# Score matmuls of a recurrent branch on column tiles of TensorE: 32 keys each, against their own group's queries

## The chip, the cores and the metric

The kernel runs on one core of a Trainium2 chip. The time is that of one execution on the device, in microseconds (us), from a timer outside the profiler; each kernel is run several times and the median is compared. The profile is one more execution, recorded by the hardware profiler: TensorE (PE in the profile; its weight loads, PEld), VectorE (DVE), ScalarE (ACT), GpSimd (POOL), and SyncE (SP), whose queue issues most of the loads.

## The reference, cut to what matters

One block of an encoder: an input projection, a recurrent branch (HGRN2) and an attention branch, a gated merge, and an MLP. The change is in the recurrent branch, 8 heads of 128 channels over 256 tokens:

```python
def hgrn2_scan(q, k, v, log_g):
    ...
    def step(S, inp):
        qc, kc, vc, gc = inp
        b = jnp.cumsum(gc, axis=2)
        o_inter = jnp.einsum('bhtk,bhkv->bhtv', qc * jnp.exp(b), S)
        diff = b[:, :, :, None, :] - b[:, :, None, :, :]
        decay = jnp.exp(jnp.where(causal[:, :, None], diff, -jnp.inf))
        scores = jnp.einsum('bhtk,bhtsk,bhsk->bhts', qc, decay, kc)
        o_intra = jnp.einsum('bhts,bhsv->bhtv', scores, vc)
        ...
```

So a query t meets each earlier key s with a decay of its own per channel. The score matrix of keys against queries is zero where s > t.

## The kernel before

All large products take their weights as float32 from HBM: ACT casts a piece to float32r (`wh`, line 91), DVE takes the rest (`wl`, line 92), and PE multiplies three times (lines 136 to 138) or, for the transposed projections, in the form of lines 178 and 183. Four `wh` and four `wl` buffers let the two engines work ahead of PE.

The recurrent branch goes by units of two heads, `n` = 0 to 3. A unit's scores are made by distance. The decay between two tokens is split at a block's border, which gives a factor to the key and a factor to the query, so that a plain matmul over the 128 channels gives the scores:

- `diagonal` (line 367): a token with itself, and a pair's second token with its first (`kk` against `q`; columns 128 to 191 of a block of `q` hold the odd tokens with their decay).
- `factors(i, B)` and `level(i, B)` for B = 2, 8, 32 (lines 376 and 407): four blocks of B tokens make a group of 4B. `kl` holds the keys, `qr` the queries: for each group 6B columns, the queries of the three later blocks seen from the block before them (3B), of two blocks seen from two before (2B), and of one block seen from three before (B).
- `level128` (line 443): the second 128 tokens against the first.

For the diagonal and the levels a unit has four blocks of 128 tokens (2 heads, NM = 2 blocks each). Before, each block is one float32 matmul of all its 128 keys against its 192 query columns (lines 371 and 415). This gives every key against every group's queries, and only the key's own group is wanted. DVE takes those out of PSUM: at the diagonal a product with the identity (line 372) and a predicated copy (line 373), at a level three predicated copies for each head (line 422), under masks that GpSimd builds at the start (line 271). They all write the score matrix `sd`, 128 keys by 128 queries for each block, which is the stationary operand of the output matmuls (line 479).

The order on PE is written in the code. The projections go on all the time, and each of their weight pieces calls `tick` (line 145), which counts down to the next entry of a list `behind`: `scores` (line 523) puts a unit's seven steps there, a few pieces apart. So a score step stands between two projection matmuls, and PE takes it in that order. The steps are: diagonal and factors of B = 2; factors of 8; level 2; factors of 32; level 8; `factors128`; level 32 and `level128`. On the other engines the scheduler of the language places the instructions.

Tiles with a tag share that tag's buffers: `e` (two) for the exponentials, `qr` (two), `kl` (three), `sm` (two PSUM buffers) for score results.

Of the kernel before, what the change touches and what calls it, by code (L numbers as in the profile page):

```python
# [50 lines left out]
def tile_hybrid_block(  # L51
# [216 lines left out]
    LEVELS = (2, 8, 32)  # L268
    mask1 = hp.tile([P, 64], F32, name="mask1")
    band(mask1, [[-2, 64]], 1)  # L270
    masks = hp.tile([P, len(LEVELS), 192], F32, name="masks")
    for i, B in enumerate(LEVELS):
        v = masks[:, i, :].rearrange("p (n k b) -> p n k b", k=6, b=B)
        for k0, k1 in ((0, 3), (3, 5), (5, 6)):
            band(v[:, :, k0:k1, :], [[-4 * B, 32 // B], [-B, k1 - k0], [0, B]], B)
    reset = hp.tile([P, 2 * T], F32, name="reset")
    nc.gpsimd.memset(reset, 1.0)
    nc.gpsimd.memset(reset.rearrange("p (c t) -> p c t", t=CH)[:, :, 0:1], 0.0)
# [47 lines left out]
    def hq_pair(u, z, g):  # L326

        nc.vector.tensor_tensor(z, z, bc(rstd_t, 1, 2), op=ALU.mult)
        s = h2(f"sq{u}")
        nc.scalar.activation(s, z, AF.Sigmoid)  # L330
        q = hp.tile([P, 2, NM, 192], F32, name=f"q{u}", tag="q", bufs=2)
        half = lambda a: a.rearrange("p h (m t) -> p h m t", t=P)
        nc.vector.scalar_tensor_tensor(q[:, :, :, 0:P], half(z), DK ** -0.5, half(s), op0=ALU.mult, op1=ALU.mult)
        odd = lambda a: a.rearrange("p h m (j u) -> p h m j u", u=2)[:, :, :, :, 1]
        for h in range(2):
            nc.vector.tensor_tensor(q[:, h, :, P:], odd(q[:, :, :, 0:P])[:, h], odd(half(g))[:, h], op=ALU.mult)
        return q

    def v_chunk(g):
# [20 lines left out]
    def hgrn_scores(n, made):  # L360

        kk, b, q = made["kk"], made["b"], made["q"]
        sd = hp.tile([P, 2, NM, P], F32, name=f"sd{n}", tag="sd", bufs=2)
        so = hp.tile([P, 2, P], F32, name=f"so{n}", tag="so", bufs=2)
        held = {}

        def diagonal():
            for h in range(2):
                ps = ps_sm.tile([P, NM, 192], F32, name=f"ps{n}_1{h}", tag="sm")
                for m in range(NM):  # L370
                    nc.tensor.matmul(ps[:, m, :], kk[:, h, m * P:(m + 1) * P], q[:, h, m, :], start=True, stop=True)
                nc.vector.tensor_tensor(sd[:, h], ps[:, :, 0:P], bc(ident, 1, NM), op=ALU.mult)
                nc.vector.copy_predicated(sd[:, h].rearrange("p m (j u) -> p m j u", u=2)[:, :, :, 1],
                                          bc(mask1.bitcast(I32), 1, NM), ps[:, :, P:])

        def factors(i, B):
            npar = 2 * T // (4 * B)
            blocks = lambda a: a.rearrange("p h t -> p (h t)").rearrange("p (n v b) -> p n v b", v=4, b=B)
            bv = blocks(b)
            end = bv[:, :, :, B - 1]  # L380
            el = hp.tile([P, npar, 4, B], F32, name=f"el{n}_{B}", tag="e", bufs=2)
            nc.vector.tensor_tensor(el, bc(end, 3, B), bv, op=ALU.subtract)
            nc.scalar.activation(el, el, AF.Exp)
            er = hp.tile([P, npar, 4, B], F32, name=f"er{n}_{B}", tag="e", bufs=2)
            rr = hp.tile([P, npar, 4], F32, name=f"rr{n}_{B}", tag=f"rr{B}", bufs=2)
            if B < CH // 2:
# [3 lines left out]
                nc.scalar.activation(rr[:, :, 1:3], rr[:, :, 1:3], AF.Exp)  # L390
# [8 lines left out]
            qr = hp.tile([P, npar, 6, B], F32, name=f"qr{n}_{B}", tag="qr", bufs=2)  # L399
            wide = lambda a, k: a.rearrange("p (a n) k b -> p a n (k b)", n=32 // B)[:, :, :, k]  # L400
            qv = q[:, :, :, 0:P].rearrange("p h m t -> p (h m) t").rearrange("p a (n w) -> p a n w", w=4 * B)
            nc.vector.tensor_tensor(wide(qr, slice(0, 3 * B)), qv[:, :, :, B:], wide(er, slice(B, 4 * B)), op=ALU.mult)
            nc.vector.tensor_tensor(qr[:, :, 3:5, :], qr[:, :, 1:3, :], bc(rr[:, :, 1:3], 3, B), op=ALU.mult)
            nc.vector.tensor_tensor(qr[:, :, 5, :], qr[:, :, 4, :], bc(rr[:, :, 1], 2, B), op=ALU.mult)
            held[i] = kl, qr, er, rr

        def level(i, B):
            kl, qr, _, _ = held[i]
            klf = kl.rearrange("p n v b -> p (n v b)")
            qrf = qr.rearrange("p n k b -> p (n k b)")  # L410
            for h in range(2):
                ps = ps_sm.tile([P, NM, 192], F32, name=f"ps{n}_{B}{h}", tag="sm")
                for m in range(NM):
                    a = 2 * h + m
                    nc.tensor.matmul(ps[:, m, :], klf[:, a * P:(a + 1) * P], qrf[:, a * 192:(a + 1) * 192],  # L415
                                     start=True, stop=True)
                dst = sd[:, h].rearrange("p m (n w) -> p m n w", w=4 * B)
                src = ps.rearrange("p m (n w) -> p m n w", w=6 * B)
                mask = masks[:, i, :].rearrange("p (n w) -> p n w", w=6 * B).bitcast(I32)
                for d0, k0, k1 in ((1, 0, 3), (2, 3, 5), (3, 5, 6)):  # L420
                    k = slice(k0 * B, k1 * B)
                    nc.vector.copy_predicated(dst[:, :, :, d0 * B:], bc(mask[:, :, k], 1, NM), src[:, :, :, k])

        def factors128():
            kl, qr, er, rr = held[2]
            heads = lambda a: a.rearrange("p (h m) v b -> p h m v b", m=NM)
            r = rr.rearrange("p (h m) v -> p h m v", m=NM)
            r0, r1 = r[:, :, 0, :], r[:, :, 1, :]
            d128 = small.tile([P, 2, 4], F32, name=f"d128{n}", tag="d128", bufs=2)
            nc.vector.tensor_copy(c128[:, :, 2], r0[:, :, 3])  # L430
            nc.vector.tensor_tensor(c128[:, :, 1], r0[:, :, 2], r0[:, :, 3], op=ALU.mult)
            nc.vector.tensor_tensor(c128[:, :, 0], c128[:, :, 1], r0[:, :, 1], op=ALU.mult)
            nc.vector.tensor_copy(d128[:, :, 1], r1[:, :, 0])
            nc.vector.tensor_tensor(d128[:, :, 2], r1[:, :, 0], r1[:, :, 1], op=ALU.mult)
# [4 lines left out]
            nc.vector.tensor_tensor(ql[:, :, 0, :], q[:, :, 1, 0:32], heads(er)[:, :, 1, 0, :], op=ALU.mult)  # L439
            nc.vector.tensor_tensor(ql[:, :, 1:4, :], heads(qr)[:, :, 1, 0:3, :], bc(d128[:, :, 1:4], 3, 32), op=ALU.mult)  # L440
            held["128"] = kc, ql

        def level128():
# [765 lines left out]
```

## Time and profile before

| | us |
|---|---|
| median of 3 runs | 1388.04 (1387.65 to 1388.07) |
| profiled execution, first to last instruction (span) | 1387.1 |
| PE busy | 1375.5 (99%) |
| DVE busy | 1137.2 (82%) |
| ACT busy | 922.2 (66%) |
| POOL busy | 143.3 (10%) |

The median lies 0.9 us above the span of the profiled execution; the timer counts a little on both sides of the span. PE's busy time is the union of its matmuls from start to modelled end; since matmuls are pipelined, a matmul's length in a row is longer than the time until the next one starts. The chain of waits counts each piece only up to the next one, so it is the chain that shows what a matmul costs in a full stream. A float32 matmul in the program is two matmul records and two weight loads in the trace (64 matmuls of line 415 and 371 stand there as 128 records). Records of 128*128 use the whole array, 128*64 half of its columns, 64*128 half of its rows.

### The profile page before, as it was taken

Reading aid. Unit: us, or ns where it says so; the run is one execution under the profiler, and the core shown is the slowest. Engines: PE = TensorE matmul, PEld = TensorE weight load, DVE = VectorE, ACT = ScalarE, POOL = GpSimd, SP = SyncE. Lnnn points to the kernel's source line nnn. Section 1 sums busy time; section 2 is a strip of 40 time slices with the busy share of each in tenths; the row PEclk is TensorE's granted clock in tenths of the full one; section 3 lists DMA queues with packets and bytes.
Section 4 is the critical chain, followed back from the end, with each engine's and each line's share of the span. In section 5 each row is a group of like instructions: output and inputs, shape, how many; then the busy total and the mean of one; then the engine's idle time right before and its main releaser. Section 6 shows DMA issues by size and latency. Waiting matters only on the chain.

```text
span 1387.1 us, 18586 instructions
## 1 busy us (share of the span) xinstructions
PE 1375.5 (99%) x6550; PEld 1144.4 (83%) x6550; DVE 1137.2 (82%) x1413; ACT 922.2 (66%) x1181; POOL 143.3 (10%) x227
## 2 busy tenths in 40 slices
PE   9999999999999999999999999999999999999997
PEld 7889888878788888888888888888888888888886
DVE  7897988876878785697998977879877888878885
ACT  6765655665676664446777766678666876668864
POOL 3000001100100000001211011200111001110200
PEclk9999999999999999999999999999999999999999
DMA  9644446685669896558979789997899888998892
GB/s 324 240 168 152 154 166 230 178 291 169 163 213 286 260 271 225 187 167 273 295 221 309 247 257 297 264 271 228 251 297 301 243 237 248 276 303 262 261 282 95
DMA packets 124077, 331.61 MB, mean 239 GB/s; under 512 B 11072, under 2 KB 11840, under 8 KB 123600
## 3 DMA queue, kind: packets, MB, share of 16 engines
q1 hardware_dynamic: 103696, 265.59, 54.6%
q0 software_dynamic: 19568, 64.04, 23.5%
q8 instruction: 51, 0.84, 0.2%
q10 hardware_dynamic: 720, 0.81, 0.2%
q14 instruction: 42, 0.34, 0.1%
HBM read 271.67 MB, written 10.49 MB: 203 GB/s over the span
## 4 chain that ended last, share of the span: by engine, by line
PE 96%; DMA 1%; ACT 1%; DVE 1%; issue 0%; SPq 0%; POOLq 0%; POOL 0%; ACTq 0%; DVEq 0%
PE acc_ak L178 2%; PE acc_hf L178 2%; PE acc_hq L178 2%; PE acc_aq L178 2%; PE ps L415 1%; PE acc_hq L183 1%; PE acc_ak L183 1%; PE tp_u L109 1%; PE acc_hf L183 1%; PE acc_hi L137 1%; PE acc_hg L137 1%; PE acc_bb L136 1%; PE acc_ba L138 1%; PE acc_hg L136 1%; PE acc_hi L138 1%; PE acc_hg L138 1%
## 5 line engine op out<-in xcount | busy, mean ns | idle before, releaser
L178 PE MATMUL acc_aq<-act_x,wh_aq 128*128 128x512 f32 x128 | 41.7, 402 | 0.0
L178 PE MATMUL acc_hf<-act_x,wh_hf 128*128 128x512 f32 x128 | 41.1, 403 | 0.0
L178 PE MATMUL acc_hq<-act_x,wh_hq 128*128 128x512 f32 x128 | 40.8, 400 | 0.0
L178 PE MATMUL acc_ak<-act_x,wh_ak 128*128 128x512 f32 x128 | 40.4, 397 | 0.0
L91 ACT CAST wh_bb<-raw_bb 128x1024 fp32r<-128x1024 f32 x16 | 16.9, 1054 | 23.3 <-PE acc_ba L138 17.7
L92 DVE TENSOR_TENSOR wl_bb<-raw_bb,wh_bb 128x1024 fp32r<-128x1024 f32 x16 | 19.6, 1223 | 14.8 <-ACT wh_bb L91 14.8
L91 ACT CAST wh_ba<-raw_ba 128x1024 fp32r<-128x1024 f32 x16 | 16.8, 1053 | 20.5 <-PE acc_bb L138 13.8
L92 DVE TENSOR_TENSOR wl_ba<-raw_ba,wh_ba 128x1024 fp32r<-128x1024 f32 x16 | 19.6, 1224 | 12.2 <-ACT wh_ba L91 12.2
L183 PEld LDWEIGHTS acc_hf<-act_x,wl_hf 128*128 128x128 f32 x128 | 23.4, 188 | 6.5 <-DVE wl_hf L92 1.4
L183 PEld LDWEIGHTS acc_hq<-act_x,wl_hq 128*128 128x128 f32 x128 | 23.4, 188 | 6.2 <-DVE wl_hq L92 1.0
L92 DVE TENSOR_TENSOR wl_aq<-raw_aq,wh_aq 128x1024 fp32r<-128x1024 f32 x16 | 19.5, 1221 | 10.8 <-ACT wh_aq L91 10.8
L91 ACT CAST wh_aq<-raw_aq 128x1024 fp32r<-128x1024 f32 x16 | 16.7, 1051 | 16.8 <-PE acc_hg L138 7.3
L183 PEld LDWEIGHTS acc_ak<-act_x,wl_ak 128*128 128x128 f32 x128 | 23.4, 188 | 5.4 <-issue 0.2
L183 PEld LDWEIGHTS acc_aq<-act_x,wl_aq 128*128 128x128 f32 x128 | 23.4, 188 | 5.0 <-issue 0.2
L183 PE MATMUL acc_aq<-act_x,wl_aq 128*128 128x256 f32 x128 | 25.8, 283 | 0.0
L92 DVE TENSOR_TENSOR act_u<-tp_u,act_u 128x512 fp32r<-128x512 f32 x32 | 21.9, 685 | 4.7 <-ACT act_u L91 4.2
L136 PE MATMUL acc_hg<-wh_hg,act_x 128*128 128x512 f32 x64 | 25.6, 400 | 0.0
L136 PE MATMUL acc_hi<-wh_hi,act_x 128*128 128x512 f32 x64 | 25.5, 399 | 0.0
L183 PE MATMUL acc_hf<-act_x,wl_hf 128*128 128x256 f32 x128 | 24.7, 280 | 0.7 <-DVE wl_hf L92 0.7
L183 PE MATMUL acc_hq<-act_x,wl_hq 128*128 128x256 f32 x128 | 24.7, 279 | 0.6 <-DVE wl_hq L92 0.6
L136 PE MATMUL acc_bb<-wh_bb,act_yb 128*128 128x512 f32 x64 | 25.2, 393 | 0.0
L137 PE MATMUL acc_hi<-wl_hi,act_x 128*128 128x512 f32 x64 | 24.9, 390 | 0.0
(1928 smaller groups left out, 5221.3 us busy)
## 6 DMA issues: line engine op xcount, KB each, us to landing
raw_hi<-in_w_in_n_dram SPq DMA_DIRECT2D x16, 512.0 KB, 3.7
raw_hg<-in_w_in_n_dram SPq DMA_DIRECT2D x16, 512.0 KB, 3.6
raw_aq<-in_w_in_t_dram SPq DMA_DIRECT2D x16, 512.0 KB, 3.8
raw_ak<-in_w_in_t_dram SPq DMA_DIRECT2D x16, 512.0 KB, 4.9
raw_ba<-in_w_branch_a_dram SPq DMA_DIRECT2D x16, 512.0 KB, 4.5
raw_bb<-in_w_branch_b_dram SPq DMA_DIRECT2D x16, 512.0 KB, 4.6
raw_hf<-in_w_in_t_dram SPq DMA_DIRECT2D x12, 512.0 KB, 3.6
raw_hq<-in_w_in_t_dram SPq DMA_DIRECT2D x12, 512.0 KB, 3.7
```

The source lines that it names most:

```text
L91: casts[:] = [(copy or nc.scalar.copy)(hi, src)]
L92: return nc.vector.tensor_tensor(lo, src, hi.bitcast(F32), op=ALU.subtract)
L109: nc.tensor.transpose(tp[:, j, :], src[:, j * P:(j + 1) * P], ident)
L136: nc.tensor.matmul(acc, hi, wh, start=first, stop=False, skip_group_check=True)
L137: nc.tensor.matmul(acc, hi, wl, start=False, stop=False, skip_group_check=True)
L138: nc.tensor.matmul(acc, lo, wh, start=False, stop=last, skip_group_check=True)
L178: nc.tensor.matmul(acc[:, cb, :], wh[:, cb * P:(cb + 1) * P], r.rearrange("p u t -> p (u t)"), start=kt == 0, stop=last)
L183: nc.tensor.matmul(acc[:, cb, 0:T], wl[:, cb * P:(cb + 1) * P], r[:, 0, :], start=False, stop=False)
L415: nc.tensor.matmul(ps[:, m, :], klf[:, a * P:(a + 1) * P], qrf[:, a * 192:(a + 1) * 192], start=True, stop=True)
```

## The change

Every group of 32 keys of a block gets its own matmul, on a column tile of TensorE: its 32 keys are the stationary operand (128 x 32), its own 48 query columns the moving one, and the result goes to that group's 32 partitions of PSUM. `q` is laid out by groups of 32 tokens and 48 columns (`[P, 16, 48]`). At the diagonal and at B = 2 and 8 this gives 16 matmuls of 48 columns in one PSUM tile `[P, 4, 48]`, where there were 4 of 192 columns in two tiles. At B = 32 a group is the whole block; its first three quarters of keys meet 96, 64 and 32 query columns, whose order in `qr` is changed for this (7 slots of 32, in a buffer of its own), so that the results already stand where the score matrix wants them.

DVE's copies for the diagonal, 2 and 8 go into a compact tile `near` (128 x 4 x 32) under compact masks (`own`, `odds`, `steps_in`). `sd` is now two fixed tiles that GpSimd clears once at the start. ACT fills them: four copies from `near` (`placed`), and three copies from PSUM at B = 32, which needs no mask any more.

```diff
-    masks = hp.tile([P, len(LEVELS), 192], F32, name="masks")
-    for i, B in enumerate(LEVELS):
+    masks = hp.tile([P, len(LEVELS) - 1, 192], F32, name="masks", tag="e", bufs=2)
+    for i, B in enumerate(LEVELS[:-1]):
...
+    QUARTERS = [slice(32 * j, 32 * j + 32) for j in range(4)]
...
+    for j, r in enumerate(QUARTERS):
+        nc.gpsimd.tensor_copy(own[r], ident[r, 32 * j:32 * j + 32])
+        nc.gpsimd.tensor_copy(odds[r], mask1[r, 16 * j:16 * j + 16])
+        nc.gpsimd.tensor_copy(steps_in[r], masks[r, :, 48 * j:48 * j + 48])
+    sds = [hp.tile([P, 2, NM, P], F32, name=f"sd{i}", tag=f"sd{i}", bufs=1) for i in range(2)]
+    for sd in sds:
+        nc.gpsimd.memset(sd, 0.0)
...
-        q = hp.tile([P, 2, NM, 192], F32, name=f"q{u}", tag="q", bufs=2)
...
-        for h in range(2):
-            nc.vector.tensor_tensor(q[:, h, :, P:], odd(q[:, :, :, 0:P])[:, h], odd(half(g))[:, h], op=ALU.mult)
+        q = hp.tile([P, 16, 48], F32, name=f"q{u}", tag="q", bufs=2)
...
+        nc.vector.tensor_tensor(q[:, :, 32:48], odd(q[:, :, 0:32]), odd(parts32(g)), op=ALU.mult)
...
+        def quarters(keys, queries, what):
+            ps = ps_sm.tile([P, 4, 48], F32, name=f"ps{n}_{what}", tag="sm")
+            for a in range(4):
+                for j, r in enumerate(QUARTERS):
+                    c = 4 * a + j
+                    nc.tensor.matmul(ps[r, a, :], keys[:, 32 * c:32 * c + 32], queries[:, 48 * c:48 * c + 48], start=True, stop=True)
+            return ps
+
         def diagonal():
-            for h in range(2):
-                ps = ps_sm.tile([P, NM, 192], F32, name=f"ps{n}_1{h}", tag="sm")
-                for m in range(NM):
-                    nc.tensor.matmul(ps[:, m, :], kk[:, h, m * P:(m + 1) * P], q[:, h, m, :], start=True, stop=True)
-                nc.vector.tensor_tensor(sd[:, h], ps[:, :, 0:P], bc(ident, 1, NM), op=ALU.mult)
-                nc.vector.copy_predicated(sd[:, h].rearrange("p m (j u) -> p m j u", u=2)[:, :, :, 1],
-                                          bc(mask1.bitcast(I32), 1, NM), ps[:, :, P:])
+            ps = quarters(kk.rearrange("p h t -> p (h t)"), q.rearrange("p j t -> p (j t)"), "1")
+            nc.vector.tensor_tensor(near, ps[:, :, 0:32], bc(own, 1, 4), op=ALU.mult)
+            nc.vector.copy_predicated(near.rearrange("p a (j u) -> p a j u", u=2)[:, :, :, 1],
+                                      bc(odds.bitcast(I32), 1, 4), ps[:, :, 32:48])
...
+            else:
+                qr = hp.tile([P, npar, 7, B], F32, name=f"qr{n}_{B}", tag="qr32", bufs=1)
...
         def level(i, B):
...
-            for h in range(2):
-                ps = ps_sm.tile([P, NM, 192], F32, name=f"ps{n}_{B}{h}", tag="sm")
-                for m in range(NM):
-                    a = 2 * h + m
-                    nc.tensor.matmul(ps[:, m, :], klf[:, a * P:(a + 1) * P], qrf[:, a * 192:(a + 1) * 192],
-                                     start=True, stop=True)
...
+            if B < 32:
+                ps = quarters(klf, qrf, B)
...
                 for d0, k0, k1 in ((1, 0, 3), (2, 3, 5), (3, 5, 6)):
                     k = slice(k0 * B, k1 * B)
-                    nc.vector.copy_predicated(dst[:, :, :, d0 * B:], bc(mask[:, :, k], 1, NM), src[:, :, :, k])
+                    nc.vector.copy_predicated(dst[:, :, :, d0 * B:], bc(mask[:, :, k], 1, 4), src[:, :, :, k])
+                return
+            ps = ps_sm.tile([P, 4, P], F32, name=f"ps{n}_{B}", tag="sm")
+            for a in range(4):
+                for v, r in enumerate(QUARTERS[:3]):
+                    c = 7 * a + 3 * v
+                    nc.tensor.matmul(ps[r, a, 32 * (v + 1):], klf[:, a * P + 32 * v:a * P + 32 * v + 32],
+                                     qrf[:, 32 * c:32 * (c + 3 - v)], start=True, stop=True)
+            for v, r in enumerate(QUARTERS[:3]):
+                nc.scalar.copy(sd4[r, :, 32 * (v + 1):], ps[r, :, 32 * (v + 1):])
+
+        def placed():
+            for j, r in enumerate(QUARTERS):
+                nc.scalar.copy(sd4[r, :, 32 * j:32 * j + 32], near[r])
...
+        def near_ones():
+            l[1]()
+            placed()
+
...
-        return (sd, so), [first, f[1], l[0], f[2], l[1], factors128, final]
+        return (sd, so), [first, f[1], l[0], f[2], near_ones, factors128, final]
```

In the order of the built program SP's instructions are the same as before. On PE each score step stands between the same two projection matmuls as before. The first one, unit 0's diagonal, stood so before (`ps_10` and `ps_11` are the results of its two heads, `acc_hi` the projection under way):

```order
L138 MATMUL acc_hi_650<-wh_hi_6_706,act_x_108 128x512
L371 MATMUL ps_10_719<-q_646,kk_636 128x192 x2
L371 MATMUL ps_11_724<-q_646,kk_636 128x192 x2
L136 MATMUL acc_hi_650<-wh_hi_6_706,act_x_108 128x512
L137 MATMUL acc_hi_650<-wl_hi_6_707,act_x_108 128x512
```

and stands so now (in the changed kernel's line numbers):

```order
L138 MATMUL acc_hi_659<-wh_hi_6_715,act_x_108 128x512
L384 MATMUL ps_1_728<-q_656,kk_646 32x48 x16
L136 MATMUL acc_hi_659<-wh_hi_6_715,act_x_108 128x512
L137 MATMUL acc_hi_659<-wl_hi_6_716,act_x_108 128x512
L138 MATMUL acc_hi_659<-wh_hi_6_715,act_x_108 128x512
```

Four matmuls over the whole array have become 16 over a quarter of its columns; nothing else moved there.

The second place is ACT at the end of the branch, where unit 3's `level128` result goes to `so` between casts of the next projection's weights (`wh_aq`). Before:

```order
L91 CAST wh_hg_14_2139<-raw_hg_14_2138 128x1024
L91 CAST wh_aq_0_2166<-raw_aq_0_2165 128x1024
L91 CAST wh_aq_4_2207<-raw_aq_4_2206 128x1024
L449 COPY so_1916<-ps_128_2128 128x256
L91 CAST wh_aq_8_2248<-raw_aq_8_2247 128x1024
```

and now:

```order
L91 CAST wh_hg_14_2277<-raw_hg_14_2276 128x1024
L455 COPY sd_421<-near_2021 32x4x32 x2
L91 CAST wh_aq_0_2304<-raw_aq_0_2303 128x1024
L455 COPY sd_421<-near_2021 32x4x32 x2
L91 CAST wh_aq_4_2345<-raw_aq_4_2344 128x1024
L451 COPY sd_421<-ps_32_2250 32x4x96
L451 COPY sd_421<-ps_32_2250 32x4x64
L451 COPY sd_421<-ps_32_2250 32x4x32
L482 COPY so_2020<-ps_128_2266 128x256
L91 CAST wh_aq_8_2386<-raw_aq_8_2385 128x1024
```

ACT's seven new copies of the unit stand between the casts; the casts keep their order.

More of the change, by code (lines that the diff above doesn't have):

```diff
@@ L275, in tile_hybrid_block @@
             band(v[:, :, k0:k1, :], [[-4 * B, 32 // B], [-B, k1 - k0], [0, B]], B)
+    QUARTERS = [slice(32 * j, 32 * j + 32) for j in range(4)]
+    own = hp.tile([P, 32], F32, name="own")
+    odds = hp.tile([P, 16], F32, name="odds")
+    steps_in = hp.tile([P, len(LEVELS) - 1, 48], F32, name="steps_in")
+    for j, r in enumerate(QUARTERS):
[5 more added lines that the diff above has]
+        nc.gpsimd.memset(sd, 0.0)
     reset = hp.tile([P, 2 * T], F32, name="reset")
@@ L330, in hq_pair @@
         nc.scalar.activation(s, z, AF.Sigmoid)
-        q = hp.tile([P, 2, NM, 192], F32, name=f"q{u}", tag="q", bufs=2)
-        half = lambda a: a.rearrange("p h (m t) -> p h m t", t=P)
-        nc.vector.scalar_tensor_tensor(q[:, :, :, 0:P], half(z), DK ** -0.5, half(s), op0=ALU.mult, op1=ALU.mult)
-        odd = lambda a: a.rearrange("p h m (j u) -> p h m j u", u=2)[:, :, :, :, 1]
-        for h in range(2):
-            nc.vector.tensor_tensor(q[:, h, :, P:], odd(q[:, :, :, 0:P])[:, h], odd(half(g))[:, h], op=ALU.mult)
+        q = hp.tile([P, 16, 48], F32, name=f"q{u}", tag="q", bufs=2)
+        parts32 = lambda a: a.rearrange("p h (j t) -> p (h j) t", t=32)
+        nc.vector.scalar_tensor_tensor(q[:, :, 0:32], parts32(z), DK ** -0.5, parts32(s), op0=ALU.mult, op1=ALU.mult)
+        odd = lambda a: a.rearrange("p j (t u) -> p j t u", u=2)[:, :, :, 1]
+        nc.vector.tensor_tensor(q[:, :, 32:48], odd(q[:, :, 0:32]), odd(parts32(g)), op=ALU.mult)
         return q
@@ L362, in hgrn_scores @@
         kk, b, q = made["kk"], made["b"], made["q"]
-        sd = hp.tile([P, 2, NM, P], F32, name=f"sd{n}", tag="sd", bufs=2)
+        sd = sds[n % 2]
+        sd4 = sd.rearrange("p h m t -> p (h m) t")
         so = hp.tile([P, 2, P], F32, name=f"so{n}", tag="so", bufs=2)
+        near = hp.tile([P, 4, 32], F32, name=f"near{n}", tag="near", bufs=2)
         held = {}
-        def diagonal():
-            for h in range(2):
-                ps = ps_sm.tile([P, NM, 192], F32, name=f"ps{n}_1{h}", tag="sm")
-                for m in range(NM):
-                    nc.tensor.matmul(ps[:, m, :], kk[:, h, m * P:(m + 1) * P], q[:, h, m, :], start=True, stop=True)
-                nc.vector.tensor_tensor(sd[:, h], ps[:, :, 0:P], bc(ident, 1, NM), op=ALU.mult)
-                nc.vector.copy_predicated(sd[:, h].rearrange("p m (j u) -> p m j u", u=2)[:, :, :, 1],
-                                          bc(mask1.bitcast(I32), 1, NM), ps[:, :, P:])
+        def quarters(keys, queries, what):
[5 more added lines that the diff above has]
+            return ps
+        def diagonal():
+            ps = quarters(kk.rearrange("p h t -> p (h t)"), q.rearrange("p j t -> p (j t)"), "1")
+            nc.vector.tensor_tensor(near, ps[:, :, 0:32], bc(own, 1, 4), op=ALU.mult)
+            nc.vector.copy_predicated(near.rearrange("p a (j u) -> p a j u", u=2)[:, :, :, 1],
+                                      bc(odds.bitcast(I32), 1, 4), ps[:, :, 32:48])
         def factors(i, B):
@@ L398, in factors @@
             nc.vector.tensor_tensor(kl, blocks(kk), el, op=ALU.mult)
[L399 to L404, printed above, removed]
+            if B < 32:
+                qr = hp.tile([P, npar, 6, B], F32, name=f"qr{n}_{B}", tag="qr", bufs=2)
+                wide = lambda a, k: a.rearrange("p (a n) k b -> p a n (k b)", a=16)[:, :, :, k]
+                qv = q[:, :, 0:32].rearrange("p a (n w) -> p a n w", w=4 * B)
+                nc.vector.tensor_tensor(wide(qr, slice(0, 3 * B)), qv[:, :, :, B:], wide(er, slice(B, 4 * B)), op=ALU.mult)
+                one, two, three, far = qr[:, :, 1:3, :], qr[:, :, 3:5, :], qr[:, :, 4, :], qr[:, :, 5, :]
+            else:
+                qr = hp.tile([P, npar, 7, B], F32, name=f"qr{n}_{B}", tag="qr32", bufs=1)
+                qv = q[:, :, 0:32].rearrange("p (a v) t -> p a v t", v=4)
+                nc.vector.tensor_tensor(qr[:, :, 0:7:3, :], qv[:, :, 1:4, :], er[:, :, 1:4, :], op=ALU.mult)
+                one, two, three, far = qr[:, :, 3:7:3, :], qr[:, :, 1:5:3, :], qr[:, :, 4, :], qr[:, :, 2, :]
+            nc.vector.tensor_tensor(two, one, bc(rr[:, :, 1:3], 3, B), op=ALU.mult)
+            nc.vector.tensor_tensor(far, three, bc(rr[:, :, 1], 2, B), op=ALU.mult)
             held[i] = kl, qr, er, rr
@@ L410, in level @@
             qrf = qr.rearrange("p n k b -> p (n k b)")
-            for h in range(2):
-                ps = ps_sm.tile([P, NM, 192], F32, name=f"ps{n}_{B}{h}", tag="sm")
-                for m in range(NM):
-                    a = 2 * h + m
-                    nc.tensor.matmul(ps[:, m, :], klf[:, a * P:(a + 1) * P], qrf[:, a * 192:(a + 1) * 192],
-                                     start=True, stop=True)
-                dst = sd[:, h].rearrange("p m (n w) -> p m n w", w=4 * B)
-                src = ps.rearrange("p m (n w) -> p m n w", w=6 * B)
-                mask = masks[:, i, :].rearrange("p (n w) -> p n w", w=6 * B).bitcast(I32)
+            if B < 32:
+                ps = quarters(klf, qrf, B)
+                dst = near.rearrange("p a (n w) -> p a n w", w=4 * B)
+                src = ps.rearrange("p a (n w) -> p a n w", w=6 * B)
+                mask = steps_in[:, i, :].rearrange("p (n w) -> p n w", w=6 * B).bitcast(I32)
                 for d0, k0, k1 in ((1, 0, 3), (2, 3, 5), (3, 5, 6)):
                     k = slice(k0 * B, k1 * B)
-                    nc.vector.copy_predicated(dst[:, :, :, d0 * B:], bc(mask[:, :, k], 1, NM), src[:, :, :, k])
+                    nc.vector.copy_predicated(dst[:, :, :, d0 * B:], bc(mask[:, :, k], 1, 4), src[:, :, :, k])
[11 more added lines that the diff above has]
+                nc.scalar.copy(sd4[r, :, 32 * j:32 * j + 32], near[r])
         def factors128():
```

4 lines of the change are left out of this document (2 added, 2 removed).

## The prediction

> **What bounds the kernel now.** The page first: busy shares, and the chain that ended last.
>
> ```profile
> PE 1375.5 (99%) x6550; PEld 1144.4 (83%) x6550; DVE 1137.2 (82%) x1413; ACT 922.2 (66%) x1181; POOL 143.3 (10%) x227
> ...
> PE 96%; DMA 1%; ACT 1%; DVE 1%; issue 0%; SPq 0%; POOLq 0%; POOL 0%; ACTq 0%; DVEq 0%
> ```
>
> PE is busy 99% of the span and is 96% of the chain. So the time is the sum of what PE streams; the question is what the change does to that sum, in the stretch where the score matmuls stand, and whether anything else is close behind PE there. The busy time by windows (span from:to, length, then busy time of PE, PEld, DVE, ACT and POOL, clock, DMA share, GB/s):
>
> ```profile
> 55.00:100.00 45.00, 45.00 (x212) 38.17 (x211) 44.05 (x93) 34.30 (x46) 0.00 (x0) 1.00 0.51 175
> 55.00:215.00 160.00, 160.00 (x835) 139.22 (x834) 142.48 (x312) 101.84 (x132) 2.38 (x2) 1.00 0.47 161
> ```
>
> From 55 to 215 us PE is never idle, at a granted clock of 1.00; DVE is at 89%, ACT at 64%, the DMA engines at 0.47. In the first 45 us of it DVE is at 98%. The chain of waits in one score step (start, length until the next piece, what):
>
> ```profile
> 111.36 0.46 PE acc_hf L178 x2
> 111.82 0.23 PE acc_hf L183 x2
> 112.06 1.30 PE ps L415 x8
> 113.36 0.46 PE acc_hf L178 x2
> 113.82 0.23 PE acc_hf L183 x2
> ```
>
> The eight records of line 415 take 1.30 us, 0.1625 each, and the projection goes on without a gap on either side: 0.46 and 0.23 before and after. So a score step costs PE what it streams and nothing else: 0.1625 us for 192 columns, or 0.846 ns a column. The groups of the stretch give how many:
>
> ```profile
> L415 PE MATMUL ps<-qr,kl 128*128 128x192 f32 x96 | 17.5, 325 | 0.0
> L371 PE MATMUL ps<-q,kk 128*128 128x192 f32 x32 | 5.8, 325 | 0.0
> ```
>
> 128 records, 16 steps of eight, 20.8 us on the path. DVE's copies behind them are not on the chain.
>
> **PE, part by part.** Removed: 16 steps of 1.30 us. Added: steps of column tiles. Only two places of this kernel, both in the attention branch, use part of the array. Line 632 uses two column tiles of 64 in turn, line 595 two row tiles of 64:
>
> ```profile
> 316.89 0.47 PE acc_aq L178 x2
> 317.36 0.11 PE acc_aq L183
> 317.47 1.45 PE pa L632 x16
> 318.92 0.32 PE acc_aq L183
> ```
>
> ```profile
> 254.84 0.46 PE acc_ak L178 x2
> 255.30 0.23 PE acc_ak L183 x2
> 255.53 0.86 PE s L595 x8
> 256.39 0.66 PE acc_ak L178 x2
> ```
>
> ```profile
> L632 PEld LDWEIGHTS pa<-pt,av x64: 132/137/137, 308.5 to 390.0; 128*64 128x64 f32 x64
> L632 PE MATMUL pa<-pt,av x64: 272/326/430, 308.5 to 390.1; 128*64 128x256 f32 x32, 128*64 128x128 f32 x32
> L595 PEld LDWEIGHTS s<-ak0T,aq0T x16: 182/187/188, 251.2 to 255.8; 64*128 64x128 f32 x16
> L595 PE MATMUL s<-ak0T,aq0T x16: 272/374/378, 251.2 to 256.0; 64*128 64x128 f32 x8, 64*128 64x256 f32 x8
> ```
>
> Line 632 has four such steps, so one step is 8 records of 256 columns and 8 of 128, 3072 columns. One after the other they would stream 3072 x 0.846 = 2.60 us. The step takes 1.45, and the matmul of line 183 behind it 0.32, where that costs 0.115 in the plain stream (0.23 for two, above): 1.45 + 0.32 - 0.115 = 1.655. So the two tiles stream side by side (1.30), and 0.355 is lost in going over to tiles and back. Line 595, half as many passes, gives 0.86 + 0.66 - 0.46 = 1.06 against 0.65: 0.41 lost. The difference of 0.055 is what the first weight load is shorter by (medians 187 and 137 ns, for 128 and 64 columns). For 32 columns I take 25 ns off: 0.33 us for a change there and back. Every score step makes one, since projections stand on both sides.
>
> How far apart two tiles start:
>
> ```profile
> 317.40 0.14 PEld L632 LDWEIGHTS pa<-pt,av 128*64 128x64 f32 x2 [0.25 <-ACT pt L620]
> ```
>
> Two loads of 132 to 137 ns cover 0.14 together, so they start about 7 ns apart.
>
> - Diagonal, B = 2 and B = 8, 12 steps: 16 matmuls, two records each, 32 records of 48 columns on four tiles. If all four stream side by side, each tile has 8 passes: 8 x 48 x 0.846 ns = 0.325, and the fourth tile starts 0.02 later. 0.325 + 0.02 + 0.33 = 0.675 instead of 1.30: 0.625 less, 7.5 us in all.
> - B = 32, 4 steps: the first tile has the longest work, 8 passes of 96 columns, 0.65. With 0.33 and 0.01 that is 0.99 instead of 1.30: 0.31 less, 1.2 us in all. `level128` behind it uses the whole array, and the way back to that is in the 0.33.
>
> Sum: 8.7 us off PE's stream; span 1387.1 - 8.7 = 1378.4, and with the 0.9 us that the median lies above the span, 1379.3.
>
> Four tiles at once, and passes under 128 columns, stand in no row. The bounds of the stream: at worst one after the other, 32 x 48 x 0.846 = 1.30 plus 0.33 (12 steps, and the like for B = 32: 5.3 us lost); at best a free change, 12 x (1.30 - 0.345) + 4 x 0.64 = 14.0 us gained. I take side by side, since two tiles do that fully, and the change's price from the nearest rows. The rows show a pass costing in proportion to its columns: 0.1625 for 192, and 0.44 for four of 128 (below, line 447), 0.110 each. The Trainium skill, TensorEngine Tiling (Array Packing), Instruction Overhead, speaks against short passes: about 60 cycles of overhead for each matmul, so that one column takes as long as 60, and no tiling factor from a dimension that is small already. If 48 columns cost here what 60 would, 12 x 8 x 12 x 0.846 ns = 1.0 us of the gain would go (1380.3); no row here is short enough to tell.
>
> **The other engines.** DVE's copies, per group:
>
> ```profile
> L422 DVE COPY_PREDICATED sd<-masks,ps 128x192 f32<-128x192 int32 x24 | 9.3, 395 | 1.2 <-PE ps L415 1.2
> L422 DVE COPY_PREDICATED sd<-masks,ps 128x128 f32<-128x128 int32 x24 | 7.1, 300 | 0.2
> L422 DVE COPY_PREDICATED sd<-masks,ps 128x64 f32<-128x64 int32 x24 | 5.7, 246 | 0.1
> L404 DVE TENSOR_TENSOR qr<-qr,rr 128x128 f32<-128x128 f32 x12 | 3.5, 293 | 0.0
> L372 DVE TENSOR_TENSOR sd<-ps,ident 128x256 f32<-128x256 f32 x8 | 3.1, 416 | 0.4 <-PE ps L371 0.4
> L373 DVE COPY_PREDICATED sd<-mask,ps 128x128 f32<-128x128 int32 x8 | 3.1, 462 | 0.0
> ```
>
> Out go 24 each of the three copies (9.3 + 7.1 + 5.7), and 3.1 + 3.1 for the diagonal: 28.3 us. In come, for each unit, a product of 128 columns (293 ns by line 404), a copy of 64 (246) and twice 96, 64 and 32 columns (at most 300 + 246 + 246): 2.1 us, 8.5 in all. DVE gets 20 us shorter. That is worth nothing in time by itself, since PE never waits here, but it takes away the one engine that was near PE: at 98% in the first 45 us. `q`'s new layout has the same elements in one instruction fewer, the slots of `qr` as many as before.
>
> ACT gets seven copies for each unit. By the rows nearest in columns:
>
> ```profile
> L449 ACT COPY so<-ps 128x256 f32<-128x256 f32 x4 | 1.5, 371 | 5.5 <-PE ps L447 5.5
> L390 ACT ACTIVATE rr<-rr 128x128 f32<-128x128 f32 x4 | 1.2, 310 | 0.0
> ```
>
> ```profile
> L620 ACT COPY pt<-tpp x16: 457/479/495, 269.1 to 388.2; 128x384 f32<-128x384 f32 x16
> ```
>
> From PSUM 384, 256 and 128 columns: 479 + 371 + 310 ns; from `near` four of 128: 4 x 310. That is 2.4 us a unit, 9.6 in all, of the 58 us that ACT idles in the stretch. The cover: `sd` and `so` must be ready when PE comes to line 479. At the end of the branch:
>
> ```profile
> 207.33 0.44 PE ps L447 x4
> ...
> 213.25 0.44 PE po L479 x4
> ```
>
> Unit 3's scores end on PE at 207.8, unit 2's outputs start at 213.2 and unit 3's later still; 1.2 us of copies ahead of `so` fit there. With the cover gone, PE would wait at most those 1.2 us a unit, 4.6 us.
>
> New waits: `placed` on ACT waits for DVE's last copy of B = 8, with casts queued behind it; `qr` of B = 32 has one buffer, so DVE's write waits for the level-32 matmuls of the unit before, with later `wl` pieces behind it. In both cases PE holds up to four buffers of weights, each two to four weight tiles of work, so a wait of one step is covered. GpSimd's work at the start (less of the masks, two clears of `sd`, small copies) lies ahead of a long idle time, and DVE needs the masks only behind unit 0's first score step:
>
> ```profile
> POOL rstd L99 <- DVE ms L98: 37.9, 2, 26.5
> ```
>
> It idles 26.5 us before line 99. I cost it at nothing; no transfer is added, and SP's order is unchanged.
>
> **The rivals.**
>
> 1. Only two tiles run at a time, as the rows show it. Then the 12 steps take 0.65 + 0.33 + 0.01 = 0.99, 0.31 less each, and B = 32 stays: 3.7 + 1.2 = 4.9 us gained, 1383.1. For it: four moving streams at once are not shown. Against it: two cost no more than one.
> 2. Slower: PE cannot be fed so many short instructions. A step has 32 matmul records and 32 weight loads in the time of a third of a microsecond. The densest the trace shows are line 632's 16 in 1.30 us. The price of an instruction that does no work in PE's sequencer:
>
> ```profile
> L415 PEldq EVENT_SEMAPHORE  x21: 51/51/51, 70.6 to 202.7; - x21
> ```
>
> If each record takes 51 ns to issue, a step takes 32 x 0.051 + 0.33 = 1.96 (0.66 more, 7.9 us), B = 32 24 x 0.051 + 0.33 = 1.55 (0.25 more, 1.0 us): 8.9 us slower, 1396.9. It decides from 33 ns a record on, where the gain is gone. Against it: two loads 7 ns apart. The Trainium skill, TensorE: Matmul & The Clock Gate, "Wait — 56ns, not 53.3ns?", gives no start closer than about 25 ns to the last however short the matmul, and about 62 ns for each where the sequencer decodes in software; by the first figure 3.3 us would be gained (1384.7), by the second 14.2 lost (1402.2). The 7 ns between tiles is closer than either.
> 3. The stretch does not get shorter, since the data's own chain or the loads then pace PE: no change, 1388.0. For it: DVE at 98% early. Against it: DVE's load falls most, and the DMA engines are half idle.
>
> **How the numbers follow.** Forecast 0.63, two at a time 0.20, issue 0.10, no change 0.07. The range reaches from 1377.6 (going over to tiles costs 0.1 us less, 16 x 0.1) to 1384.8: the second case, with line 595's 0.41 for the change in place of 0.33 (16 x 0.08), and the 0.4 us by which the runs of before differ. 0.17 is left out. About 0.2% (2.8 us) is what a measurement of this kernel tells from no change: below 1385.2 is faster, 0.83; 0.07 the same; slower 0.10.
>
> **What would show it.** In the chain after, a step of 32x48 should take about 0.47 with 0.2 on the matmul behind it, and the projection matmuls around it 0.23 as before. Rival 1 shows as 0.8 in such a step, rival 2 as 1.6 or more. If PE has gaps before a step or before line 479's outputs, a cover failed; if PE's stream is shorter by 9 us and the span is not, rival 3.

## The result, and the profile after

The changed kernel takes 1380.04 us (median of 4 runs, 1378.16 to 1380.89), the kernel before 1387.99 (4 runs, 1387.65 to 1388.07): a ratio of 0.9941, 95% interval 0.9927 to 0.9955. It is faster, by 8.0 us in the medians; 1379.3 was forecast. The profile after is of a run of 1380.89 us with a span of 1379.1.

The page's first lines, busy shares and the chain by engine:

```profile
PE 1367.0 (99%) x6902; PEld 1129.5 (82%) x6902; DVE 1122.4 (81%) x1353; ACT 931.3 (68%) x1209; POOL 146.0 (11%) x232
...
PE 93%; DMA 3%; DVE 2%; ACT 1%; issue 1%; SPq 0%; ACTq 0%; POOLq 0%; POOL 0%; DVEq 0%
```

PE is still 99% busy and almost the whole chain. By windows, with the columns as before (the branch now ends 8 us earlier, so the second window is shorter):

```profile
55.00:100.00 45.00, 45.00 (x309) 36.30 (x308) 43.97 (x93) 38.14 (x55) 0.00 (x0) 1.00 0.58 177
55.00:207.00 152.00, 152.00 (x1190) 125.85 (x1189) 127.64 (x252) 110.80 (x160) 2.37 (x2) 1.00 0.55 170
```

PE is never idle in the branch, as before, and streams 8 us less. DVE is still at 98% in the first 45 us, though its work there became less.

The chain in a score step, level 2 of unit 0:

```profile
72.28 0.23 PE acc_hi L138
72.51 0.48 PE ps L384 x32
72.99 0.43 PE acc_hi L136
73.42 0.24 PE acc_hi L137
```

The step takes 0.48 us where it took 1.30, and the projection matmul behind it (line 136) 0.43 in place of 0.23: 0.68 us in all. The `x32` are the 32 records of the 16 matmuls. The chain at level 32 of unit 0, which goes over to `level128` (line 480) on the whole array:

```profile
94.08 0.23 PE acc_hg L138
94.31 0.78 PE ps L448 x15
95.09 0.64 PE ps L480 x4
95.73 0.23 PE acc_hg L136
```

0.78, and 0.64 where `level128` took 0.44: 0.98 in all, instead of 1.30. The timeline in a slice of 40 ns at the start of the step of level 2 shows four matmuls under way at once:

```profile
72.44 0.25 PE L384 MATMUL ps<-qr,kl 128*32 128x48 f32 x4
```

The records of the score matmuls, from the rows of the tile `ps` (lengths in ns as minimum, median, maximum; first and last start in us):

```profile
L384 PE MATMUL ps<-qr,kl x256: 206/206/230, 72.4 to 192.1; 128*32 128x48 f32 x128
L384 PE MATMUL ps<-q,kk x128: 206/206/230, 63.6 to 179.8; 128*32 128x48 f32 x128
L448 PE MATMUL ps<-qr,kl x96: 196/219/270, 94.2 to 198.5; 128*32 128x96 f32 x32, 128*32 128x64 f32 x32, 128*32 128x32 f32 x32
```

256 + 128 records of 48 columns in 12 steps, and 96 in four. A record is 206 ns long, five times the time until its tile's next one, so the records' length says nothing of the cost here. In the trace a tile starts its next pass (the streaming of one record's columns) 42 to 43 ns after the last, its second one 67 ns after the first, and the four tiles start 6 to 7 ns apart.

DVE's groups, and then ACT's:

```profile
L442 DVE COPY_PREDICATED near<-steps_in,ps 128x96 f32<-128x96 int32 x8 | 2.2, 278 | 0.5 <-PE ps L384 0.5
L442 DVE COPY_PREDICATED near<-steps_in,ps 128x64 f32<-128x64 int32 x8 | 1.8, 228 | 0.1
L442 DVE COPY_PREDICATED near<-steps_in,ps 128x32 f32<-128x32 int32 x8 | 1.7, 210 | 0.1
L390 DVE COPY_PREDICATED near<-odds,ps 128x64 f32<-128x64 int32 x4 | 1.2, 302 | 0.0
L389 DVE TENSOR_TENSOR near<-ps,own 128x128 f32<-128x128 f32 x4 | 1.2, 290 | 0.2 <-PE ps L384 0.2
```

```profile
L91 ACT CAST wh_hf<-raw_hf 128x1024 fp32r<-128x1024 f32 x8 | 8.4, 1051 | 4.0 <-PE acc_hg L138 2.9 <-ACT sd L455 0.6 <-PE acc_hq L178 0.6
L451 ACT COPY sd<-ps 32x384 f32<-32x384 f32 x4 | 1.9, 468 | 3.1 <-PE ps L448 3.1
L451 ACT COPY sd<-ps 32x256 f32<-32x256 f32 x4 | 1.5, 365 | 0.0
L451 ACT COPY sd<-ps 32x128 f32<-32x128 f32 x4 | 1.0, 258 | 0.0
```

DVE's copies take 8.1 us (28.3 before), ACT's new ones 9.2.

To compare kernels apart from their starts and ends, I take the stretch from the first matmul of the projection `hf1`, ahead of all score steps, to the first one of `aq0`, behind them. The timeline of PE at its two ends, before:

```profile
31.08 0.50 PE L178 MATMUL acc_hf<-act_x,wh_hf 128*128 128x512 f32 x1
...
211.71 0.39 PE L178 MATMUL acc_aq<-act_x,wh_aq 128*128 128x512 f32 x1
```

and after:

```profile
31.29 0.50 PE L178 MATMUL acc_hf<-act_x,wh_hf 128*128 128x512 f32 x1 [0.67 <-DVE f L191]
...
203.37 0.39 PE L178 MATMUL acc_aq<-act_x,wh_aq 128*128 128x512 f32 x1
```

180.63 us before, 172.08 after: 8.55 less, and from 55 us on PE is never idle in either. The rest of the two spans' difference (8.0) is 0.6 of it given back elsewhere: 0.2 at the start and 0.4 in the long stages behind, where single profiles differ by as much.

### The profile page after: what moved, and what is told of

It is laid out like the page before. It is cut to its first block, busy times and chain, and to the rows that moved or that the text cites. A ratio compares the mean times of both kernels' runs of the same rounds, so it can differ in the third digit from the quotient of the medians.

```text
span 1379.1 us, 19243 instructions
## 1 busy us (share of the span) xinstructions
PE 1367.0 (99%) x6902; PEld 1129.5 (82%) x6902; DVE 1122.4 (81%) x1353; ACT 931.3 (68%) x1209; POOL 146.0 (11%) x232
## 4 chain that ended last, share of the span: by engine, by line
PE 93%; DMA 3%; DVE 2%; ACT 1%; issue 1%; SPq 0%; ACTq 0%; POOLq 0%; POOL 0%; DVEq 0%
PE acc_ak L178 2%; PE acc_aq L178 2%; PE acc_hf L178 2%; PE acc_hq L178 2%; DMA rawp_dn30r<-in_w_down_dram 1%; PE acc_hg L136 1%; PE acc_hi L136 1%; PE acc_ak L183 1%; PE acc_hi L137 1%; PE acc_hg L137 1%; PE acc_hg L138 1%; PE acc_hi L138 1%; PE acc_ba L138 1%; PE acc_bb L136 1%; PE acc_bb L138 1%; PE acc_ba L137 1%
## 5 line engine op out<-in xcount | busy, mean ns | idle before, releaser
L92 DVE TENSOR_TENSOR wl_hf<-raw_hf,wh_hf 128x1024 fp32r<-128x1024 f32 (+2 forms) x21 | 20.4, 972 | 8.6 <-ACT wh_hf L91 8.4
```

The costliest lines, as they stand in the source:

```text
L92: return nc.vector.tensor_tensor(lo, src, hi.bitcast(F32), op=ALU.subtract)
```

## The experiments

The theory: PE's stream sets the time; a score step costs the passes of its longest tile, since the tiles stream side by side, and 0.33 us for going over to tiles and back. The rivals: DVE's relief gave the gain; the number of instructions counts, not the columns; the loss of 0.33 belongs to the tiles' own work. Each time below is a median, beside that of the kernel before on the same chip; the stretch is from each kernel's own profile. The changed kernel was not timed on the chip of `tiles64`, `halves`, `merge2` and `mergeall` (before: 1387.57), so there only the stretch compares with it closely.

| kernel | us | before | ratio, 95% interval | stretch, us |
|---|---|---|---|---|
| before | | 1387.99 | | 180.63 |
| changed | 1380.04 | 1387.99 | 0.9941 (0.9927 to 0.9955) | 172.08 |
| again | 1379.73 | 1387.62 | 0.9944 (0.9931 to 0.9956) | 172.06 |
| dve_less | 1387.30 | 1387.62 | 0.9996 (0.9987 to 1.0005) | 180.62 |
| dve_more | 1380.56 | 1387.62 | 0.9947 (0.9933 to 0.9960) | 173.68 |
| jmajor | 1386.21 | 1387.62 | 0.9989 (0.9980 to 0.9998) | 178.95 |
| tiles64 | 1382.35 | 1387.57 | 0.9961 (0.9946 to 0.9976) | 176.08 |
| halves | 1382.04 | 1387.57 | 0.9960 (0.9946 to 0.9973) | 174.67 |
| merge2 | 1378.29 | 1387.57 | 0.9932 (0.9920 to 0.9945) | 170.79 |
| mergeall | 1381.24 | 1387.57 | 0.9955 (0.9943 to 0.9968) | 172.51 |
| after2 | 1378.88 | 1387.91 | 0.9935 (0.9923 to 0.9947) | 172.02 |
| merge2b | 1378.30 | 1387.91 | 0.9928 (0.9916 to 0.9940) | 170.82 |
| mergeall2 | 1374.51 | 1387.91 | 0.9902 (0.9887 to 0.9917) | 167.81 |

**The spread (again, after2).** No edit.

> The changed kernel once more, unchanged, to see how far its runs spread: its first four runs lie 2.7 us apart (1378.2 to 1380.9), those of before 0.4. If PE's stream sets the time, its runs come out 8 to 9 us under those of before, 1379 to 1380; if a part of the gain is lost late in the kernel in some runs only, single runs again lie 1 to 2 us off.

Four of the five runs lie within 1379.3 to 1379.9, one at 1382.57; the kernel before, in 21 runs on that chip, spreads from 1386.9 to 1389.5. So that the first runs of before lay within 0.4 us was luck, and a median of a few runs is good to about 1 us. The stretch comes out the same to 0.02 us. The second repeat:

> The changed kernel unchanged, on the same chip, to compare with: 1379.7, the stretch 172.1.

1378.88, and 172.02. The gain in medians is 8.0, 7.9 and 9.0 us in the three pairs of measurements.

**Is it DVE? (dve_less, dve_more).** The kernel before without its level copies:

```diff
-                    nc.vector.copy_predicated(dst[:, :, :, d0 * B:], bc(mask[:, :, k], 1, NM), src[:, :, :, k])
+                    if B == 1:
+                        nc.vector.copy_predicated(dst[:, :, :, d0 * B:], bc(mask[:, :, k], 1, NM), src[:, :, :, k])
```

> The kernel before, with full-array score matmuls, but without the predicated copies of the three levels (line 422, 22.1 us of DVE in the trace), so the score matrix holds only its diagonal part. Theory (PE's stream sets the time): no change, 1388.0, within 0.5 us. Rival (the gain came from the work taken off DVE): as much as the change gave, about 1380.

The first 45 us of the branch, in the columns of the windows above:

```profile
55.00:100.00 45.00, 45.00 (x211) 38.20 (x210) 41.38 (x79) 34.60 (x47) 0.00 (x0) 1.00 0.52 177
```

DVE is busy 41.38 us there where it was busy 44.05, and PE 45.00 as before. 22 us off DVE leave the stretch as it was to 0.01 us, and the ratio's interval holds 1. DVE's relief alone is worth nothing. And the changed kernel with the copies made five times:

```diff
-                    nc.vector.copy_predicated(dst[:, :, :, d0 * B:], bc(mask[:, :, k], 1, 4), src[:, :, :, k])
+                    for _ in range(5):
+                        nc.vector.copy_predicated(dst[:, :, :, d0 * B:], bc(mask[:, :, k], 1, 4), src[:, :, :, k])
```

> The changed kernel with each predicated copy of B = 2 and 8 made five times, 23 us more work on DVE, about as much as the change took off it. Theory: PE does not wait for these copies, 1380.0, at most 1 us more. Rival (DVE's relief is what counts): the gain goes, about 1388.

The stretch is 1.6 us longer, the time 0.8 more than `again`'s. The list of PE's waits names it:

```profile
PE ps L449 <- DVE near L443: 1.6, 1, 1.6
```

One matmul of line 449 waits once, for a copy that has yet to free a PSUM buffer. So the gain does not hang on DVE's relief. But 23 us of work put back on these copies show on PE in one place: my "nothing" for DVE was right in this direction by a margin of one wait.

**Side by side (jmajor, tiles64, halves).** The loops exchanged:

```diff
-            for a in range(4):
-                for j, r in enumerate(QUARTERS):
+            for j, r in enumerate(QUARTERS):
+                for a in range(4):
```

> The changed kernel with the two loops of a score step of B = 1, 2 and 8 exchanged: all four matmuls of the first column tile, then all four of the second, and so on. The same 16 matmuls, another order. If each tile had a long queue of its own, the step stays at 0.34 us of stream and the time at 1380. If matmuls start strictly in program order, the tiles work one after the other: 1.30 us of stream, 0.96 more in 12 steps, 1391.5. In between, if a tile takes in about one matmul ahead of the one it is working on: the next tile starts about 0.2 us after the one before, 0.95 us a step, 7 us more, 1387.

The chain at level 2 of unit 0:

```profile
71.80 1.06 PE ps L384 x32
72.86 0.43 PE acc_hi L136
```

1.06 against 0.48, and the same 0.43 behind it. In the trace the first loads of the four tiles start at 71.73, 71.93, 72.13 and 72.33 us: 0.2 us apart, as the middle case had it. The stretch is 6.9 us longer. When the second tile starts, the first one has started five of its eight passes: it works on its third matmul, and the fourth must have been taken in. This fits the middle case: a tile's neighbour starts only when the matmuls ahead of it in the program have been taken in, and a tile takes in about one matmul beyond the one that it works on. The side-by-side stream hangs on the order in which the program names the tiles.

Two tiles of 64 keys:

```diff
-            ps = ps_sm.tile([P, 4, 48], F32, name=f"ps{n}_{what}", tag="sm")
+            ps = ps_sm.tile([P, 4, 96], F32, name=f"ps{n}_{what}", tag="sm")
             for a in range(4):
-                for j, r in enumerate(QUARTERS):
-                    c = 4 * a + j
-                    nc.tensor.matmul(ps[r, a, :], keys[:, 32 * c:32 * c + 32], queries[:, 48 * c:48 * c + 48], start=True, stop=True)
-            return ps
+                for j, r in enumerate((slice(0, 64), slice(64, 128))):
+                    c = 2 * a + j
+                    nc.tensor.matmul(ps[r, a, :], keys[:, 64 * c:64 * c + 64], queries[:, 96 * c:96 * c + 96], start=True, stop=True)
+            return ps[:, :, 0:48]
```

> The changed kernel with two tiles of 64 keys in place of four of 32 for the diagonal, levels 2 and 8: 8 matmuls of 96 columns each (DVE still reads the first 48 columns, so half of the keys get the wrong group's scores). Theory (tiles stream side by side, a pass costs by its columns): 8 passes of 96 columns, 0.65 us and 0.355 for the change over, 1.0 against 0.67 a step: 4 us slower than the changed kernel, 1384. If the number of instructions counted instead, half as many would make it faster than 1380.

```profile
71.75 0.81 PE ps L384 x16
72.56 0.43 PE acc_hi L136
```

0.81 + 0.20 = 1.01 a step, and the stretch 4.0 us longer, as expected. The median, 1382.35, is 1.7 us under the 1384 of the expectation. Half as many instructions made it slower: the longest tile's columns count.

Each matmul in two of 24 columns:

```diff
-                for j, r in enumerate(QUARTERS):
+                for w, j, r in ((w, j, r) for w in (0, 24) for j, r in enumerate(QUARTERS)):
                     c = 4 * a + j
-                    nc.tensor.matmul(ps[r, a, :], keys[:, 32 * c:32 * c + 32], queries[:, 48 * c:48 * c + 48], start=True, stop=True)
+                    if True:
+                        nc.tensor.matmul(ps[r, a, w:w + 24], keys[:, 32 * c:32 * c + 32],
+                                         queries[:, 48 * c + w:48 * c + w + 24], start=True, stop=True)
```

> The changed kernel with each 48-column matmul cut into two of 24 columns, the four tiles in turn: the same columns, twice the instructions (64 records a step). If a pass costs by its columns alone: 16 x 20 ns, the same time. If the 7 ns between the starts of neighbouring tiles is what an instruction pair takes to issue, a round of four takes 28 ns where its columns take 20 to 23: 0.45 us a step instead of 0.34, 1.3 us slower. If a pass had a floor near 48 columns' time: 16 x 42 = 0.68 a step, 4 us slower, 1384.

```profile
71.51 0.68 PE ps L385 x50
72.19 0.43 PE acc_hi L136
```

0.20 us more a step, 2.6 in the stretch: between the second and third case. In this step's trace a tile starts its next 24-column pass 32 ns after the last, where the columns' share is 20. From about the 34th record on, the records come in pairs, a pair every 16 to 17 ns; that is nearly the same pace, 9.3 ns a record against 8.6 ahead of it. Sixteen passes at 32 to 33 ns and 0.33 for going over are 0.85 of the step's 0.88. So passes do have a floor, below 48 columns. The changed kernel's level 32 agrees: its third tile has passes of 32 columns, 27 ns by their number, and never starts two less than 31 ns apart. A fixed price of 8 ns for each record is less likely, since the two records of a pair start 0 to 3 ns apart. What sets the floor was not tried.

**The price of going over (merge2, mergeall, mergeall2, merge2b).** Level 2 at level 8's place:

```diff
         def near_ones():
+            l[0]()
             l[1]()
...
-        return (sd, so), [first, f[1], l[0], f[2], near_ones, factors128, final]
+        return (sd, so), [first, f[1], lambda: None, f[2], near_ones, factors128, final]
```

> The changed kernel with the matmuls of level 2 moved to the place of level 8, so that PE goes over to tiles three times a unit instead of four. Theory (each change there and back costs 0.33 us): 4 x 0.33 = 1.3 us less than the changed kernel, 1378.7. Rival (the loss is a part of the tile matmuls themselves, not of the change over): the same as the changed kernel.

The chain at the joint step of unit 0:

```profile
81.49 0.82 PE ps L384 x64
82.31 0.43 PE acc_hg L136
```

Two steps' work in 0.82 and one 0.20, where two steps take 2 x 0.68: 0.34 less. The stretch is 1.3 us shorter. The repeat beside the changed kernel:

> Levels 2 and 8 in one step once more, on the same chip as the changed kernel: the stretch 170.8 and the time 1.3 us under the changed kernel's.

The stretch is 1.2 shorter again; the medians are only 0.6 apart, within what they are good for. All tile matmuls of a unit in its last step, level 32 with PSUM room from another pool (the cut leaves this out, and the emptied steps):

```diff
+            if ps is None:
+                ps = ps_sm.tile([P, 4, 48], F32, name=f"ps{n}_{what}", tag="sm")
...
+            held["both"] = ps_sm.tile([P, 2, 4, 48], F32, name=f"ps{n}_1", tag="sm")
+            ps = quarters(kk.rearrange("p h t -> p (h t)"), q.rearrange("p j t -> p (j t)"), "1", held["both"][:, 0])
...
         def final():
+            diagonal()
+            l[0]()
+            l[1]()
             l[2]()
+            placed()
             level128()
```

> The changed kernel with all tile matmuls of a unit in its last step: diagonal, levels 2, 8 and 32 behind each other, one change there and back a unit. Theory: 12 x 0.33 = 4.0 us less than the changed kernel, 1376. Rival: the copies of DVE and ACT then come all at once, behind the last matmul, and PE or the weight casts wait for them; then less than 2 us of it arrives, with gaps on PE behind the score steps.

The rival had the size: the stretch is 0.4 us longer than the changed kernel's, not 4 shorter. The wait it named is not quite the one that came. The chain in unit 0, and PE's longest wait in the list:

```profile
91.78 0.52 PE ps L385 x32
92.30 0.02 issue
92.33 0.30 DVE near L391
92.63 0.02 issue
92.65 0.31 DVE near L392
92.96 0.04 issue
93.00 0.55 PE ps L385 x32
93.55 0.47 PE ps L450 x13
```

```profile
PE ps L385 <- DVE near L392: 4.0, 4, 3.0
```

In the middle of the step a matmul waits for DVE's two copies of the diagonal (lines 391 and 392). It writes level 2 into the same PSUM tile that those copies read: 4.0 us in four waits, the longest 3.0, in unit 2, where DVE works on other things between that step's matmuls and the copies. The last version gives all matmuls their PSUM room and issues them ahead of DVE's first copy (the cut shows it against `mergeall`):

```diff
+        def products():
+            held["ps1"] = quarters(kk.rearrange("p h t -> p (h t)"), q.rearrange("p j t -> p (j t)"), "1")
+            both = ps_sm.tile([P, 2, 4, 48], F32, name=f"ps{n}_2", tag="sm")
+            for i, B in enumerate(LEVELS[:-1]):
+                held["ps", i] = quarters(held[i][0].rearrange("p n v b -> p (n v b)"),
+                                         held[i][1].rearrange("p n k b -> p (n k b)"), B, both[:, i])
...
         def final():
-            diagonal()
-            l[0]()
-            l[1]()
+            products()
             l[2]()
-            placed()
             level128()
+            diagonal()
+            l[0]()
+            l[1]()
+            placed()
```

> One change over a unit again, but with all of a unit's tile matmuls issued ahead of DVE's first copy and with PSUM room for all of them (level 2 and 8 share a tile, level 32 has one of the other pool), so that no matmul waits for a copy. If the missing gain of the first try was only that wait (PE waited 4.0 us for DVE's diagonal copies), the stretch from hf1 to the first aq matmul takes 4.0 us less than in the changed kernel, 168.1, and the whole 1376. If the copies that come all at once hold up PE by themselves, it stays near 172 again, with PE waiting at the casts or the outputs.

```profile
91.46 1.16 PE ps L385 x96
92.61 0.64 PE ps L456 x15
93.25 0.64 PE ps L488 x4
93.90 0.23 PE acc_hg L136
```

The diagonal and levels 2 and 8 run through in 1.16 (96 records), level 32 follows in 0.64, and only `level128` pays for the way back. The stretch is 4.2 us shorter than the changed kernel's, and the time 4.4 (1374.51 against 1378.88 on the same chip). The copies still come all at once there and PE does not wait for them, so what `mergeall` lost was the wait for the PSUM tile. This is the fastest version: 1.0% under the kernel before.

## Why the prediction was right

By its steps:

- **What bounds the kernel.** Right. `dve_less` takes 22 us off DVE and the time stays; the stretch falls by what PE streams less.
- **The terms of the sum.** A step of 48 columns was put at 0.675 and takes 0.68; level 32 at 0.99 and takes 0.98. The sum, 8.7, is 8.55 in the stretch; 0.15 is not placed.
- **Four tiles at once.** Right, though the trace of before showed only two. A step of 32 passes of 48 columns in 0.35 us of stream (0.68 - 0.33) allows nothing else, `tiles64` doubles that part as it should, and the first two rivals' steps (0.8, 1.6 and more) do not occur. Rival 1 is out, and with it rival 2: 32 records every 11 ns, where it needed 32 or more (the prediction's 33 is a slip: 12 x 32 + 4 x 24 records would have to use up 16 x 0.97 us).
- **0.33 for going over.** Right: a merged step saves 0.34 in the chain, and `mergeall2`, which drops 12 of 16, saves 4.2 us, 0.35 each. The starts in the changed kernel's step of level 2 place it: the first tile starts 0.09 us later behind the projection's last matmul than the next projection matmul would, its second pass comes 0.025 late, and on the way back the first projection matmul comes 0.09 late and the second 0.11; 0.02 is the fourth tile's later start.
- **The rule on short matmuls.** The Trainium skill, TensorEngine Tiling (Array Packing), Instruction Overhead, would make 48 columns as dear as 60, an estimated 51 ns by the rows of before. A pass takes 42 to 43, near the 41 of its columns. `halves` shows a floor, but at 32 ns. The Trainium skill, TensorE: Matmul & The Clock Gate, "Wait — 56ns, not 53.3ns?", gives no start closer than about 25 ns to the last. On one tile the traces agree (32 for 24 columns), from tile to tile they do not (6 to 7).
- **DVE and ACT.** Their terms came out as priced (DVE 8.1 us in, forecast 8.5; ACT 9.2, forecast 9.6), and none is on the path. One reading failed: DVE's 98% in the first 45 us, which I took for nearness to PE and as a point for rival 3. It is 98% after too, with less to do; without the level copies it is 92% (41.38 of 45 us) and nothing is gained. DVE works ahead of PE there: PE is never idle in these 45 us in any of the three kernels.
- **From span to median.** This term was mis-sized. The later runs of before each have their span beside them: 1387.46 with 1385.6, so 1.9 us lie around the span, and 1.8 for the changed kernel (1380.89 with 1379.1). My 0.9 came from a profiled execution that was, by this, itself about 0.9 slower than the median run. As the sum took 8.7 off the same execution, the two errors cancel: it amounts to the median less 8.7. The 0.7 between forecast and result is then the 0.15 above and the scatter of the rest, which the three gains of 7.9 to 9.0 show. That the forecast came within 0.7 is in part luck.

## What to carry to other kernels

Where PE's chain is unbroken, a matmul's price is the time to the next one in the chain, not its record's length, and nothing another engine is spared counts. If only blocks on the diagonal of a product are wanted, put them on column tiles, name the tiles in turn in the program, and gather the tile work, since each trip from the whole array to tiles and back cost a third of a microsecond here. A gathered step should have PSUM room for all its results before the first copy; here it waited for the copies where it had not.

## What the runs showed of the hardware that was not expected

- The two passes of a float32 matmul on one tile do not keep its neighbours waiting: at the start of a step the four tiles' first passes stand ahead of any second one. At level 32 the third tile (32 columns) runs up to three passes ahead of the first one (96 columns). By then it has started both passes of its third matmul, which the program names behind the first tile's second, still under way. So starts are not in program order across tiles.
- The look-ahead fits about one matmul a tile: with the tiles named one after the other they start 0.2 us apart (`jmajor`), and 6.9 of the 8.55 us are gone.
- Short passes on a tile: 82 to 83 ns for 96 columns, 56 for 64, 42.5 for 48, and then a floor: 31 to 32 at the least for 32, and 32 for 24. What sets the floor is open.
